# A two-layer backbone with 32 experts: layer 0's experts placed by rank, its router in batches

## The chip, the cores and the metric

The kernel runs on one core of a Trainium2 chip. The metric is the device time of one execution in microseconds (us); before the change its median is 3009.55 us over three runs (3004.5 to 3014.62).

## The reference

A stream of 512 latent tokens and 256 context tokens, 1024 wide, passes through two layers. Each layer has a modulated RMS norm, one input projection, three token mixers (a bidirectional recurrence, full attention, windowed attention), a gated sum, an output projection with a gated residual, and then the part that matters here:

```python
h2 = rms_norm(x, norm2_g) * (1 + scale) + shift        # modulation by c or c_ctx
group  = argmax(h2 @ w_group)                           # 1 of 4 groups
top2   = two largest of (h2 @ w_router) in that group   # 2 of 8 experts, softmax weights
y      = sum over the two: w * (silu(h2 @ gate_e) * (h2 @ up_e)) @ down_e
x      = x + gate * y
```

The group's softmax probability is a factor of the weights too. An expert has gate and up matrices of 1024 x 512 and a down matrix of 512 x 1024, all fp32. The output is the final norm of the 512 latent tokens. Layer 0 runs its experts for all 768 tokens, layer 1 for the 512 latent ones.

## The kernel before

**Router.** `out_proj` (lines 1075 to 1156) runs the output projection in two halves of 512 columns, over six token tiles in layer 0 and four in layer 1, three matmuls per k (tile `oo`). The second half's results are normalised in pairs of tiles; transposes (`xgt`) and logits (`lg`) are put off in a queue `steps`, of which `run(1)` takes one step per tile, and the rest of the router (`h2_out`, `route`, `route_pos`, `route_tab`) lies in a queue `later`, run after the last tile. For each token and choice the router works out the expert (`Er`), the token's position among that expert's tokens (`pos`, a matmul with a triangle of ones), and by a one-hot matrix `po` (L1317) a table `tab` (L1318) of 128 rows with the token number and the weight for each place. `ridx` (L1153) is that table as indices. The normalised rows go to DRAM (`h2D`): ScalarE scales, GpSimd adds the shift row (L1196), a DMA writes (L1198); the last tile's add is on VectorE (L1193), and its DMA on SyncE.

**Quads.** The experts run in eight quads. Quad q holds expert q of each of the four groups; each of these four has one of TensorE's four tiles of 32 columns. A plane gives each of the four 32 rows, so it is one gather of 128 rows of `h2D` (L1509, GpSimd), eight transposes, 64 gate matmuls, 64 up matmuls, a Silu (L1555) and a product, four transposes, 64 down matmuls (L1549), and a scatter that adds 128 rows to `xsD` in DRAM (L1514). `PLANES = (3, 2)` gives layer 0 three planes for every quad (96 places per expert) and layer 1 two (64). Tokens beyond that go through a loop at L1454 whose number of turns is read from `nx` into a register at L1453; it runs no turn here.

The order of work in a quad is: gate (both halves of the weights), down of the quad before, Silu, up, transposes of the next. Successive matmuls are written for the four column tiles in turn (`quad_mm`, `quad_down`); the order in which an engine gets its instructions is fixed when the kernel is built.

**Weights.** Each layer has 192 loads of 1 MiB, in the order of use, all on SyncE's queue (`ring_load`, L989). They fill slots in turn: 15 in layer 0, 16 in layer 1 (`wraw`, `pf`, `wspr`, `ring`). A load waits until TensorE has read what the slot held. The first 15 or 16 are issued during the projection and the router.

## Time and profile before

| | before |
|---|---|
| median of three runs | 3009.55 us |
| profiled execution | 3010.81 us, its span 3009.0 us |
| mean granted clock of TensorE | 0.972 |
| TensorE busy | 2822.9 us (94%) |
| VectorE, ScalarE, GpSimd busy | 1270.4, 835.1, 370.3 us |
| layer 0: last projection matmul, indices, quads left | 1024.9, 1070.3, 1699.1 us |
| layer 1: the same | 2446.4, 2475.6, 2976.9 us |

The busy time of an engine is the sum of its instructions, overlaps counted once. Matmuls are pipelined, so TensorE that is busy all the time need not run at its peak: the number of matmuls in a stretch tells more. "PEclk" is the granted clock, 1.00 is 2.4 GHz. "DMA share" is the mean busy share of the core's 16 DMA engines. In a timeline a row can gather several instructions of one kind (x8); the brackets behind it give the engine's idle time and what ended it. Names ending in q, as SPq, are an engine's instruction queue.

### The profile page before, as it was taken

How to read it: one execution, taken by the hardware profiler on the slowest of the kernel's cores; microseconds unless marked ns; L12 is line 12 of the kernel's file. 1: busy time of each engine (PE TensorE's matmuls, PEld its weight loads, DVE VectorE, ACT ScalarE, POOL GpSimd, SP SyncE). 2: the span in 40 equal slices, each digit the busy share in tenths (PEclk: the TensorE clock that was granted, in tenths of full speed). 3: DMA queues.
4: the chain of work that ended last, by engine and by line, in shares of the span. 5: the costliest groups of instructions: out<-in, count | busy, mean ns of one | idle time of the engine just before them, and what ended most of it. 6: DMA issues, size and time to landing. Idle time of an engine off the chain costs nothing. (4 is left out here: it accounts for less than half of the span.)

```text
span 3009.0 us, 49938 instructions
## 1 busy us (share of the span) xinstructions
PE 2822.9 (94%) x20898; PEld 1924.1 (64%) x20898; DVE 1270.4 (42%) x2693; ACT 835.1 (28%) x1706; POOL 370.3 (12%) x463
## 2 busy tenths in 40 slices
PE   6999999999999879999999799999999969999995
PEld 5999998888999733343333388888887853333321
DVE  5667555464446622221111356666566651110001
ACT  5322345555422200000000243335666221000000
POOL 1000221012212201111100100011001220100000
PEclk9999999999999889999999899999999979999998
DMA  6232334034555568998787612222112768999995
GB/s 237 70 112 96 119 105 138 25 104 169 189 206 191 199 255 342 385 377 353 290 326 293 227 50 74 91 95 75 48 40 82 272 248 358 409 416 414 416 414 198
DMA packets 198654, 640.07 MB, mean 213 GB/s; under 512 B 21585, under 2 KB 87377, under 8 KB 149273
## 3 DMA queue, kind: packets, MB, share of 16 engines
q1 hardware_dynamic: 165960, 552.59, 47.3%
q0 software_dynamic: 31744, 81.58, 8.7%
q8 instruction: 166, 2.72, 0.4%
q10 hardware_dynamic: 720, 2.66, 0.2%
q14 instruction: 64, 0.52, 0.0%
HBM read 600.44 MB, written 57.26 MB: 219 GB/s over the span
## 5 line engine op out<-in xcount | busy, mean ns | idle before, releaser
L503 PE MATMUL ga<-hhi,wsp 128*128 128x384 f32 (+1 forms) x1152 | 355.2, 372 | 4.4 <-ACT gt L950 2.8
L1537 PE MATMUL gu<-ring,xT 128*32 128x512 f32 x1824 | 331.1, 599 | 8.8 <-DMA ring<-in_w_exp_up 6.9
L1537 PE MATMUL gu<-wspr,xT 128*32 128x512 f32 x1328 | 290.2, 600 | 5.1 <-DMA wspr<-in_w_exp_up 3.9
L1537 PE MATMUL gu<-wraw,xT 128*32 128x512 f32 x1488 | 264.2, 604 | 1.6 <-DMA wraw<-in_w_exp_up 1.5
L1549 PE MATMUL dn<-ring,hT 128*32 128x512 f32 x1128 | 232.6, 595 | 0.0
L239 DVE TENSOR_TENSOR wsp<-wraw,wsp 128x1024 fp32r<-128x1024 f32 x148 | 183.3, 1241 | 115.4 <-ACT wsp L238 107.5
L503 PEld LDWEIGHTS ga<-hhi,wsp 128*128 128x128 f32 x1152 | 210.0, 189 | 23.5 <-ACT gt L950 4.4
L238 ACT ACTIVATE wsp<-wraw 128x1024 fp32r<-128x1024 f32 x148 | 155.9, 1058 | 176.6 <-PE bp L1026 89.9
L1537 PEld LDWEIGHTS gu<-ring,xT 128*32 128x32 f32 x1824 | 89.6, 110 | 177.7 <-issue 151.7
L503 PE MATMUL ga<-hlo,wsp 128*128 128x384 f32 (+1 forms) x576 | 191.3, 359 | 0.0
L1549 PE MATMUL dn<-wspr,hT 128*32 128x512 f32 x688 | 173.8, 596 | 0.0
L1026 PE MATMUL bp<-bhl,wsp 128*128 128x384 f32 (+1 forms) x864 | 167.7, 355 | 1.0 <-ACT bhl L1007 1.0
L1026 PEld LDWEIGHTS bp<-bhl,wsp 128*128 128x128 f32 x864 | 153.8, 188 | 14.5 <-issue 1.2
L1514 POOL DMA_INDIRECT xsD<-yr,ridx x40 | 63.5, 1588 | 761.8 <-DVE yr L1578 526.1
L1537 PE MATMUL gu<-pf,xT 128*32 128x512 f32 x480 | 155.0, 599 | 1.2 <-DMA pf<-in_w_exp_up 1.2
L245 PE MATMUL aacc<-wsp,hhi 128*128 128x256 f32 x512 | 149.9, 293 | 2.1 <-ACT gt L950 1.1
L1537 PEld LDWEIGHTS gu<-wraw,xT 128*32 128x32 f32 x1488 | 68.6, 111 | 123.5 <-issue 113.6
L1578 DVE SCALAR_TENSOR_TENSOR yr<-dn,wts,G 128x512 f32<-128x512 f32 x48 | 35.6, 749 | 260.4 <-PE dn L1549 231.8
L246 PE MATMUL aacc<-wsp,hhi 128*128 128x256 f32 x512 | 144.2, 282 | 0.7 <-DVE wsp L239 0.7
L1559 DVE TENSOR_TENSOR hs<-hs,gu 128x512 f32<-128x512 f32 x40 | 27.5, 687 | 277.8 <-PE gu L1537 270.9
L247 PE MATMUL aacc<-wsp,hlo 128*128 128x256 f32 x512 | 143.9, 282 | 0.0
L888 ACT ACTIVATE P<-S,nm 128x768 f32<-128x768 f32 (+3 forms) x160 | 120.4, 752 | 78.4 <-DVE nm L886 36.6
(352 smaller groups left out, 5536.9 us busy)
## 6 DMA issues: line engine op xcount, KB each, us to landing
ring<-in_w_exp_down SPq DMA_DIRECT2D x57, 1024.0 KB, 20.6
ring<-in_w_exp_up SPq DMA_DIRECT2D x51, 1024.0 KB, 15.0
wraw<-in_w_mod SPq DMA_DIRECT2D x46, 1024.0 KB, 7.7
wraw<-in_w_in SPq DMA_DIRECT2D x42, 1024.0 KB, 4.8
wraw<-in_w_exp_gate SPq DMA_DIRECT2D x40, 1024.0 KB, 13.7
ring<-in_w_exp_gate SPq DMA_DIRECT2D x39, 1024.0 KB, 22.9
wspr<-in_w_exp_gate SPq DMA_DIRECT2D x34, 1024.0 KB, 19.1
wraw<-in_w_exp_up SPq DMA_DIRECT2D x34, 1024.0 KB, 15.4
```

Source lines behind the costliest of these rows:

```text
L238: self.nc.scalar.activation(hv, src, AF.Copy)
L239: (self.nc.gpsimd if len(parts) in slow else self.nc.vector).tensor_tensor(lv, src, hv.bitcast(F32), op=OP.subtract)
L245: mm(out, l[0], r[0], start=start, stop=False)
L246: mm(out, l[0], r[1], start=False, stop=False)
L247: mm(out, l[1], r[0], start=False, stop=stop)
L503: mm(o, w(k)[wi][:, fs], self.h[hi_][:, k, a:a + s], start=k == 0 and wi == 0 and hi_ == 0, stop=k == 7 and wi == 1)
L888: nc.scalar.activation(P[:, :nk], S[:, :nk], AF.Exp, bias=nm[:, 0:1], accum_out=nm[:, 2:3])
L1026: nc.tensor.matmul(o[:, c, :step], w(k)[wi][:, fs], b[:, 4 * hi + k, c * step:(c + 1) * step], start=k == 0 and wi == 0 and hi == 0, stop= ...
L1514: self.nc.gpsimd.indirect_dma_start(out=self.xsD[L][:, :], out_offset=bass.IndirectOffsetOnAxis(ap=idx, axis=0), in_=y[:, :], in_offset=No ...
L1537: self.nc.tensor.matmul(o[c], xT[n][:, 4 * h + k, c], w(g, k), start=h + k == 0, stop=h * k == 3)
L1549: self.nc.tensor.matmul(b[c], h[:, k, c], w[k // 2](g, k % 2)[:, js], start=k == 0, stop=k == 3)
L1578: V.scalar_tensor_tensor(y[:, js], b, wt, G, op0=OP.mult, op1=OP.mult)
```

## The change

- **Ranks.** In layer 0 the experts of a group are placed in quads by rank: expert 0 stays in quad 0, and the others follow by falling number of tokens. The counts come from a matmul (`route_count`), the ranks from comparisons (`route_rank`). The table of the rank's owner, `ids`, is made by three operations on one partition and a cast.
- **Planes.** Layer 0 gets three planes in quads 0 to 2 and two in the rest, 19 instead of 24. Layer 1 keeps two. Tokens over 96 or 64 go to the overflow loop, now in blocks of 128.
- **Weights.** Layer 0's loads of quads 1 to 7 take the expert's number from a register of SyncE, one per place, 28 in all, read from `ids`. Quad 0's loads stay fixed.
- **Router.** It works on three tiles (two in layer 1) at a time. Logits of all tiles but the last are taken inside the projection's loop, and the first half's position matmuls too. The table matmuls come at the end: twelve in layer 0.
- **Rows of `h2D`.** The shift rows are written to DRAM beforehand; ScalarE scales in place, and a DMA that accumulates adds the rows. GpSimd's and VectorE's additions go.

```diff
-PLANES = (3, 2)
+PLANES = ((3, 3, 3, 2, 2, 2, 2, 2), (2,) * QUADS)
+CAP = 2 * UNIT
...
+        if i == 7:
+            ctx = CTX if L < DEPTH - 1 else 0
+            for a, r0, r1 in ((1, 0, ctx), (0, ctx, ctx + SEQ)):
+                if r1 > r0:
+                    row = self.modrow(L, a, 3)
+                    src = bass.AP(tensor=row.tensor, offset=row.offset, ap=[[0, r1 - r0], [1, D]])
+                    nc.gpsimd.dma_start(self.h2D[L][1 + r0:1 + r1, :], src)
...
+            def src(g):
+                if L or q == 0:
+                    e = w[8 * g + q]
+                else:
+                    if (q, g) not in self.ev:
+                        r = 4 * q + g
+                        self.ev[q, g] = self.nc.sync.value_load(self.ids[:1, r:r + 1], min_val=0, max_val=N_EXP - 1)
+                    e = w[bass.ds(self.ev[q, g], 1)].rearrange("a d f -> (a d) f")
...
                     for k in range(8):
                         self.mm3(b[:, :512], tuple(x[:, k, i * 128:(i + 1) * 128] for x in self.m), w(k), k == 0, k == 7)
+                        if k == 4:
+                            if half == 1 and i == nt - 1:
+                                self.route_pos(0, cut, R)
+                            run(2 if half == 1 and i == 1 else 1 if half or i > 1 else 0)
                     run(1)
...
+            self.h2_out(L, nt - 1, nt, R)
+            self.route(L, cut, nt, R)
+            self.route_pos(cut, nt, R)
+            if L == 0:
+                self.route_rank(p)
+            self.route_tab(L, cut if L else 0, nt, R)
...
+    def h2_out(self, L, i0, i1, R):
+        nc = self.nc
+        for i in range(i0, i1):
+            x = R["x"][self.ot[i]]
+            nc.scalar.activation(x, x, AF.Copy, scale=R["r"][:, i:i + 1])
+            nc.gpsimd.dma_start(self.h2D[L][i * 128 + 1:i * 128 + 129, :], x, accum_op=OP.add)
...
+        V.tensor_tensor(key, self.cnt, c[:, C_KM:C_KM + 32], op=OP.mult)
+        V.tensor_tensor(key, key, c[:, C_KC:C_KC + 32], op=OP.add)
+        g = p.tile([128, 32, 8], F32, name="kgt", tag="g2")
+        kg = key.rearrange("p (g j) -> p g j", j=8)
+        for i in range(4):
+            V.tensor_tensor(g[:, 8 * i:8 * i + 8], kg[:, i:i + 1].to_broadcast([128, 8, 8]), kg[:, i, :, None].to_broadcast([128, 8, 8]), op=OP.is_gt)
+        V.tensor_reduce(self.rk, g, axis=AX.X, op=OP.add)
...
-            order = [(q, n) for q in range(QUADS) for n in range(P)]
+            order = [(q, n) for q in range(QUADS) for n in range(P[q])]
...
-                S = [self.ps.tile([128, 512], F32, name="gu", tag="gu", bufs=6) for _ in range(P)]
+                S = [self.ps.tile([128, 512], F32, name="gu", tag="gu", bufs=6) for _ in range(P[q])]
```

Three places show how instructions move. On TensorE after layer 0's last out-projection matmul (`oo`), before, from the end of the logits (`lg`) to the first transpose of a gathered tile (`xtp`):

```order
L1206 MATMUL xgt<-cst,xo_9795 128x128 x4
L1214 MATMUL lg<-wr,xgT 128x36 x4
L1206 MATMUL xgt<-cst,xo_9797 128x128 x4
L1214 MATMUL lg<-wr,xgT 128x36 x8
L1277 MATMUL pos<-Ep,cst 128x64
L1279 MATMUL pos<-Es,cst 128x64
L1318 MATMUL tab<-rh,po 128x48 x4
L1277 MATMUL pos<-Ep,cst 128x64
L1279 MATMUL pos<-Es,cst 128x64
L1318 MATMUL tab<-rh,po 128x48 x4
```

and of the change, from inside the last tile's projection on:

```order
L1340 MATMUL pos<-Ep,cst 128x96
L1342 MATMUL pos<-Es,cst 128x96
L1262 MATMUL xgt<-cst,xo_9804 128x128 x4
L254 MATMUL oo<-wsp,mhi 128x512
L255 MATMUL oo<-wsp,mhi 128x512
L256 MATMUL oo<-wsp,mlo 128x512
```

```order
L1270 MATMUL lg<-wr,xgT 128x36 x4
L1262 MATMUL xgt<-cst,xo_9806 128x128 x4
L1270 MATMUL lg<-wr,xgT 128x36 x4
L1340 MATMUL pos<-Ep,cst 128x96
L1342 MATMUL pos<-Es,cst 128x96
L1358 MATMUL cnt<-Ep,cst 128x32
L1411 MATMUL tab<-rh,po 128x48 x12
L1626 MATMUL xtp<-cst,xo_9244 128x128 x8
```

Three rounds of positions and four table matmuls have become one round inside the projection, one after it, and twelve table matmuls at the end. On VectorE of the change, from the ranks (`rk`) to the one-hot matrices (`po`):

```order
L1374 SCALAR_TENSOR_TENSOR rk<-rk,cst 128x32
L1391 TENSOR_TENSOR Xr<-Er,rk 128x384
L1216 TENSOR_TENSOR idq<-rk,cst 1x1024
L1392 TENSOR_REDUCE rt<-Xr 128x12
L1217 TENSOR_TENSOR idq<-idq,cst 1x1024
L1394 TENSOR_TENSOR gq<-rt,cst 128x108
L1218 TENSOR_REDUCE idf<-idq 1x32
L1396 TENSOR_TENSOR Eq<-gq 128x96
```

The three operations of 1024 elements for `ids` stand among those that make the table. On SyncE, before, behind the last tile's rows:

```order
L1198 DMA h2D_95<-xo_9795 128x1024
L989 DMA ring<-in_w_exp_up 128x2048 x3
L989 DMA wraw<-in_w_exp_up 128x2048
L989 DMA wraw<-in_w_exp_gate 128x2048 x3
L989 DMA pf_9778<-in_w_exp_gate 128x2048
```

and of the change:

```order
L988 ISA x2
L1554 TENSOR_LOAD nx
L1554 ISA x2
L1019 DMA wraw<-in_w_exp_up 128x2048
L1019 ISA
L1019 DMA wraw<-in_w_exp_gate 128x2048
L1019 ISA
L1019 DMA wraw<-in_w_exp_gate 128x2048
```

The 28 reads of `ids` and the read of `nx` stand ahead of the first load that needs a freed slot, and each load by register has an instruction of its own beside it.

## Rows read from the trace of the kernel before

**Rows 1.** Stretches, experts: span, busy by engine (count), PEclk, DMA share, GB/s.

```profile
1081.00:1710.00 629.00, 612.80 (x4910) 216.15 (x4908) 116.35 (x207) 46.89 (x76) 59.28 (x47) 0.99 0.84 323
2488.00:2977.00 489.00, 467.70 (x3251) 153.70 (x3252) 51.22 (x102) 27.84 (x47) 34.44 (x26) 0.99 0.96 393
```

**Rows 2.** The same columns for windows of 100 us within these stretches.

```profile
1200.00:1300.00 100.00, 99.76 (x872) 35.68 (x876) 22.04 (x59) 9.45 (x16) 11.32 (x10) 1.00 0.98 394
1500.00:1600.00 100.00, 95.97 (x727) 32.69 (x722) 14.46 (x22) 5.92 (x10) 4.92 (x4) 0.98 0.78 301
2800.00:2900.00 100.00, 95.39 (x630) 30.02 (x630) 10.15 (x14) 4.56 (x8) 6.27 (x4) 1.00 1.01 411
```

**Rows 3.** Timeline of ScalarE, first Silu of a quad: start, us, instruction.

```profile
1098.66 0.60 ACT L1555 ACTIVATE hs<-gu 128x512 f32<-128x512 f32 x1 [12.76 <-PE gu L1537]
1147.82 0.60 ACT L1555 ACTIVATE hs<-gu 128x512 f32<-128x512 f32 x1 [2.99 <-PE gu L1537]
1217.79 0.60 ACT L1555 ACTIVATE hs<-gu 128x512 f32<-128x512 f32 x1 [2.93 <-PE gu L1537]
1288.99 0.60 ACT L1555 ACTIVATE hs<-gu 128x512 f32<-128x512 f32 x1 [2.93 <-PE gu L1537]
1443.62 0.60 ACT L1555 ACTIVATE hs<-gu 128x512 f32<-128x512 f32 x1 [3.29 <-PE gu L1537]
1616.82 0.60 ACT L1555 ACTIVATE hs<-gu 128x512 f32<-128x512 f32 x1 [13.27 <-PE gu L1537]
2849.83 0.60 ACT L1555 ACTIVATE hs<-gu 128x512 f32<-128x512 f32 x1 [10.83 <-PE gu L1537]
2912.78 0.60 ACT L1555 ACTIVATE hs<-gu 128x512 f32<-128x512 f32 x1 [14.65 <-PE gu L1537]
```

**Rows 4.** Line 1453, TensorE weight queue: ns min/median/max, first to last start.

```profile
L1453 PEldq EVENT_SEMAPHORE  x12: 51/51/51, 1699.1 to 2976.9; - x12
```

**Rows 5.** Columns as in rows 1: two down products of layer 0.

```profile
1230.00:1250.00 20.00, 20.00 (x192) 6.93 (x188) 8.86 (x12) 0.00 (x0) 3.64 (x2) 1.00 0.84 298
1460.00:1480.00 20.00, 20.00 (x129) 5.95 (x125) 6.43 (x9) 0.00 (x0) 2.59 (x2) 1.00 0.62 231
```

**Rows 6.** Line 1453 and timeline, SyncE: register read, first later loads.

```profile
L1453 SPq TENSOR_LOAD <-nx x2: 306/389/472, 1672.5 to 2952.1; - x2
...
1094.38 0.33 SPq L989 DMA_DIRECT2D wraw<-in_w_exp_up  x1
1095.18 1.60 SPq L989 DMA_DIRECT2D wraw<-in_w_exp_gate  x3
```

**Rows 7.** Timeline after layer 0's last out-projection matmul, TensorE, VectorE, GpSimd.

```profile
1024.46 0.40 PE L247 MATMUL oo<-wsp,mlo 128*128 128x512 f32 x1
1024.69 0.98 PE L1214 MATMUL lg<-wr,xgT 128*128 128x36 f32 x8
1025.50 1.07 PE L1206 MATMUL xgt<-cst,xo 128*128 128x128 f32 x8
1068.07 1.94 PE L1318 MATMUL tab<-rh,po 128*128 128x48 f32 x8 [2.85 <-DVE po L1317]
...
1032.97 2.80 DVE L1236 SCALAR_TENSOR_TENSOR t<-l,gm,cst 128x4 f32<-128x4 f32 x1
1053.28 1.28 DVE L1193 SCALAR_TENSOR_TENSOR xo<-xo,n2y,S 128x1024 f32<-128x1024 f32 x1
1070.27 0.18 DVE L1153 TENSOR_TENSOR ridx<-tab,z 128x24 int32<-128x24 f32 x1
...
1033.39 2.35 POOL L1196 TENSOR_TENSOR xo<-xo,S 128x1024 f32<-128x1024 f32 x1
```

**Rows 8.** Timeline, layer 1: last out-projection matmul, indices.

```profile
2445.96 0.40 PE L247 MATMUL oo<-wsp,mlo 128*128 128x512 f32 x1
...
2475.57 0.17 DVE L1153 TENSOR_TENSOR ridx<-tab,z 128x16 int32<-128x16 f32 x1
```

**Rows 9.** DMA issues of layer 0's experts: name, queue, count, median us to landing.

```profile
xsD<-yr,ridx POOLq DMA_INDIRECT x24, 8.3
```

More of the change, by code (lines that the diff above doesn't have):

```diff
@@ L36 @@
 UNIT = 32
[L37 removed]
 QUADS = 8
[L39 to L40 removed]
+PLANES = ((3, 3, 3, 2, 2, 2, 2, 2), (2,) * QUADS)
+CAP = 2 * UNIT
+BLOCK = 128
+MAX_EXTRA = 2 * T // (CAP + 1)
 FAR = float(1 << 20)
@@ L50 @@
 C_GO = C_R32 + 32
-C_W = C_GO + 32
+C_RK = C_GO
+C_KM = C_RK + 32
+C_KC = C_KM + 32
+C_GR = C_KC + 32
+C_W = C_GR + 32
 def host_consts():
@@ L1096, in out_proj @@
             R["ss"] = p.tile([128, NT, 2], F32, name="ssx")
+            R["r"] = p.tile([128, NT], F32, name="rn")
+            R["SW"] = p.tile([128, NT, 36], F32, name="SWt")
+            R["pl"] = p.tile([128, 2 * NT, 3], F32, name="plt")
+            R["pp"] = p.tile([128, 2 * NT], F32, name="ppt")
             R["tb"] = self.ps.tile([128, 512], F32, name="tab", tag="bg", bufs=1)
             wo = self.I["w_out"][L]
-            steps, later = deque(), deque()
+            steps = deque()
+            cut = nt // 2
+            sw = p.tile([2, 36], F32, name="sw")
             def run(k):
                 for _ in range(k):
-                    q = steps or later
-                    if q:
-                        q.popleft()()
+                    if steps:
+                        steps.popleft()()
             def logit_bias():
@@ new lines, in route @@
+        E = self.Er[:, i0:i1]
+        src = sel
+        v = []
+        for k in range(2):
+            v.append(tl([1], f"v{k}"))
+            V.reduce_max(v[k][:, :, 0], src, axis=AX.X)
+            q, m = tl([32], f"k{k}"), tl([1], f"m{k}")
+            V.tensor_tensor(q, src, bc(v[k], [32]), op=OP.is_equal)
+            V.tensor_tensor(q, q, bc(c[:, None, C_R32:C_R32 + 32], [32]), op=OP.mult)
+            V.reduce_max(m[:, :, 0], q, axis=AX.X)
+            V.tensor_tensor(E[:, :, k], q, bc(m, [32]), op=OP.is_equal)
+            if k == 0:
+                src = tl([32], "sel2")
@@ L1293, in route_pos @@
[L1293 to L1299 removed]
+        nc.tensor.matmul(b[:, :32 * n], c[:, C_TRI:C_TRI + 128], R["Es", i0].rearrange("p a e -> p (a e)"), start=False, stop=True)
@@ new lines, in route_pos, with route_count @@
+        V.tensor_tensor(R["pl"][:, 2 * i0:2 * i1], ge[:, :, 0:3], ge[:, :, 1:4], op=OP.subtract)
+        V.tensor_reduce(pn[:, :, 0], ge[:, :, 1:4], axis=AX.X, op=OP.add)
+        V.scalar_tensor_tensor(R["pp"][:, 2 * i0:2 * i1], pn[:, :, 0], -float(UNIT), pos, op0=OP.mult, op1=OP.add)
+    def route_count(self):
+        b = self.ps.tile([128, 512], F32, name="cnt", tag="tp")
+        self.nc.tensor.matmul(b[:, :32], self.c[:, C_ONE:C_ONE + 128], self.Ep[:, len(self.ot)], start=True, stop=True)
+        self.nc.vector.tensor_copy(self.cnt, b[:, :32])
@@ new lines, in route_rank @@
+    def route_rank(self, p):
+        V = self.nc.vector
+        c = self.c
+        self.route_count()
+        key = p.tile([128, 32], F32, name="key")
+        V.tensor_tensor(key, self.cnt, c[:, C_KM:C_KM + 32], op=OP.mult)
[5 more added lines that the diff above has]
+        V.tensor_reduce(self.rk, g, axis=AX.X, op=OP.add)
+        V.scalar_tensor_tensor(self.rk, self.rk, 4.0, c[:, C_GR:C_GR + 32], op0=OP.mult, op1=OP.add)
@@ L1314, in route_tab @@
-        for a in range(2):
-            for ch in range(2):
-                po = p.tile([128, 128], F32, name="po", tag="po", bufs=4)
-                V.tensor_scalar(po, c[:, C_IO:C_IO + 128], self.tgt[:, i + a, ch:ch + 1], None, op0=OP.is_equal)
-                nc.tensor.matmul(R["tb"][:, :48], po, rh[:, a, ch].rearrange("p a b n -> p (a b n)"),
-                                 start=i + a + ch == 0, stop=last and a + ch == 2)
+        n = i1 - i0
+        m = 2 * n
+        last = i1 == len(self.ot)
@@ new lines, in route_tab, with tl @@
+        bufs = 1 if L == 0 else 2
+        w = 2 * NT if L == 0 else 4
+        def tl(shape, name):
+            return p.tile([128, w] + shape, F32, name=name, tag=name, bufs=bufs)[:, :m]
+        rt = self.rt[:, 2 * i0:2 * i1]
+        rk = c[:, C_RK:C_RK + 32] if L else self.rk
+        X = tl([32], "Xr")
+        V.tensor_tensor(X, self.Er[:, i0:i1].rearrange("p a c e -> p (a c) e"), rk[:, None, :].to_broadcast([128, m, 32]), op=OP.mult)
+        V.tensor_reduce(rt, X, axis=AX.X, op=OP.add)
@@ new lines, in route_tab @@
+        V.tensor_tensor(rh[:, :, 1], Df, self.wt2[:, i0:i1].rearrange("p a c -> p (a c)")[:, :, None].to_broadcast([128, m, QUADS * 3]),
+                        op=OP.mult)
+        for a in range(m):
+            po = p.tile([128, 128], F32, name="po", tag="po", bufs=4)
+            V.tensor_scalar(po, c[:, C_IO:C_IO + 128], tgt[:, a:a + 1], None, op0=OP.is_equal)
+            nc.tensor.matmul(R["tb"][:, :48], po, rh[:, a].rearrange("p b n -> p (b n)"),
+                             start=i0 + a == 0, stop=last and a == m - 1)
@@ L1431, in moe @@
                     self.quad_down(L, p, hT, q - 1, need)
-                hs_ = [self.exp_s(S[n], 128) for n in range(P)]
-                U = [self.ps.tile([128, 512], F32, name="gu", tag="gu", bufs=6) for _ in range(P)]
+                hs_ = [self.exp_s(S[n], 128) for n in range(P[q])]
+                U = [self.ps.tile([128, 512], F32, name="gu", tag="gu", bufs=6) for _ in range(P[q])]
                 self.quad_mm(U, xT, need((1, q, 0)), 0)
@@ L1436, in moe @@
                 if q + 1 < QUADS:
-                    xT = [next_x() for _ in range(P)]
+                    xT = [next_x() for _ in range(P[q + 1])]
                 prev = [self.exp_m(h, u, 128) for h, u in zip(hs_, U)]
```

267 lines of the change are left out of this document (133 added, 134 removed).

## The prediction

> **What bounds the kernel now.** I read the table of stretches first. The experts of layer 0 (1081 to 1710 us) are the longest stretch that the change touches: TensorE is busy 612.8 of 629 us and the DMA engines are busy 0.84 of the time [rows 1]. The same eight quads in layer 1, with two planes instead of three, take 489 us at a DMA share of 0.96. The 100 us windows say it more sharply [rows 2]: in 2800:2900 the DMA share is 1.01 at 411 GB/s with TensorE idle for 4.6 us, in 1200:1300 both are nearly full, in 1500:1600 TensorE has no time left and the DMA is at 0.78. So layer 1 waits for weights, and layer 0 starts with both close to their limits and ends with TensorE alone as the bound.
>
> The timeline of the Silu, one per plane as soon as a quad's gate matmuls are done, gives the pace [rows 3]. Layer 0's first Silus of quads 0, 1, 2, 3, 5 and 7 stand at 1098.66, 1147.82, 1217.79, 1288.99, 1443.62 and 1616.82: steps of 49.2, 70.0 and 71.2, then 154.6 and 173.2 for two quads each, 77 and 87 for one. TensorE leaves the quads at 1699.1 [rows 4], 82.3 after the last of them: 600.4 in all. Layer 1 goes at 62.9 (2849.83 to 2912.78) and leaves 64.2 after its last Silu, at 2976.9.
>
> Why do layer 0's late quads take 77 to 87 and not 71? In 1230:1250 TensorE does 192 matmuls in 20 us, in 1460:1480 only 129, both at full clock [rows 5]. The first are the down products of an early quad, written so that successive matmuls go to the four column tiles in turn; in the late ones the built order puts several for one tile behind each other (two or three with the same weight slot). The late order costs 192 x (20/129 - 20/192) = 9.8 us for a three-plane down product. That accounts for most of the 6 to 16.
>
> **The planes.** The change takes 5 of 24 planes from layer 0, all in quads 3 to 7. A step from Silu q to Silu q+1 holds down(q-1), up(q) and gate(q+1), so I go step by step.
> - 0 to 1 and 1 to 2 keep three planes everywhere and the built order of before: 49.2 and 70.0.
> - 2 to 3 loses one plane of gate(3), 64 matmuls at 9.6 per us, 6.7, and eight transposes, some 1.6: 71.2 - 8.3 = 62.9.
> - 3 to 4 has two planes of up and gate but down(2) of three, now in the slow order: 192/6.45 = 29.8; 256 matmuls at 8 per us (my estimate between the two rates of [rows 5]) 32.0; transposes about 5. That is 66.8.
> - 4 to 5, 5 to 6, 6 to 7 and what follows have the work of layer 1, whose built order of column tiles they also have. There the step is 62.9 and the tail 64.2. Layer 0 has 15 weight slots and layer 1 has 16, so that a load can be issued a little later; I take 64.5 and 65.
>
> The sum is 49.2 + 70.0 + 62.9 + 66.8 + 3 x 64.5 + 65 = 507.4, against 600.4: 93 us less. From the low side, if weights never were late, a two-plane step would be the 62.9 of layer 1 less the 21.3 us that its TensorE is idle in 489, spread on eight quads: 60.2, and 15 us more gain. From the high side, if two-plane quads in layer 0 took the 70.0 of its own three-plane step, the sum would be 49.2 + 70.0 + 70 + 72 + 3 x 70 + 70 = 541: a gain of 59.
>
> A rule speaks against 62.9. The windows of layer 1 move 411 GB/s [rows 2], and 24 loads of 1 MiB at that rate are 61.2 us, close to the step. The Trainium skill's page "DMA: Bandwidth & Descriptors" (Specifications) gives about 358 GB/s as the limit of HBM for one core; by it 24 loads would take an estimated 70.3 us and the gain would be the 59 of the high side. The trace does not agree with it, in any window of layer 1, so I leave that case a chance and do not take it.
>
> **Weights by register.** From quad 1 on, layer 0's loads take their expert from one of 28 registers, filled from the table of ids by SyncE. Before has a read of this kind: 306 to 472 ns at L1453 [rows 6], with two short instructions behind it; with these I count 0.65 us, so 28 are 18 us. They stand behind the ids, some 8 us before the indices of the gathers, and behind them stands only the load for the first slot to come free. Before issues that load 24.1 us after the indices are ready (1094.38 against 1070.27). From ids to that load there are then 32 us for 18 us of reads: they cost nothing. Were that cover gone, each us late would idle the DMA queue by a us, at most 18. The read of the overflow count moves ahead of these loads too; its value is ready soon after the indices. Each load gets one more register instruction. Three loads without it take 1.60 us to issue (0.53 each); with a whole register read on each of them, the nearest row, it would be 1.2 us, or 28 us for 24 loads, still under the 63 us of a quad. From below it costs nothing. I take nothing.
>
> **The router in layer 0.** The last out-projection matmul ends at 1024.86, the indices come at 1070.27 [rows 7]: 45.4 us. Eight sets of logits stand behind that matmul in before; in after only one does. The other seven run inside the projection, where TensorE is saturated, so they push its end out by 7 x (0.81 + 0.53) = 9.4 us (a logit set from 1024.69 to 1025.50; four transposes at half of 1.07 for eight). Behind it I count from the built order: three vector operations of 0.69 and then transposes, copy and logits, 5.4; some 26 dependent small vector operations at about 0.2, 5.2; positions 1.1; the rank (13 operations) 3.4; from there to the first one-hot matrix 6.9, of which three operations of 1024 elements on one partition are 3.8 by the nearest row, the 1.28 at 1053.28; twelve table matmuls at 1.94/4 each, 5.8; the last two operations and their wait 1.9. Sum 29.7. What goes are the additions on GpSimd, 2.35 each [rows 7], beside which VectorE's 128x4 operations take 2.80 instead of 0.2. The gain is 45.4 - 9.4 - 29.7 = 6.3. From the low side, if each small operation cost 0.4, it is -2; from the high side, with 0.15, about 9. One wait is new: the position matmuls of tiles 0 to 2 stand inside the last projection tile, and its remaining matmuls queue behind them. After the routing of these tiles is issued TensorE has 36 matmuls of 0.23 [rows 7] and three logit sets before them, 12 us; VectorE has about 32 small operations and two output tiles, 10 to 11. I take no stall, and up to 5 us as the end.
>
> **The router in layer 1.** From 2446.36 to 2475.57 are 29.2 us [rows 8]. Five sets move into the projection, 6.7; behind it the same chain without the rank and with four table matmuls is about 18. Gain 4.5, with -3 and 7 as ends. The rows of the last tile are now added to DRAM by an accumulating transfer: the nearest row is the accumulating scatter, 8.3 us to landing [rows 9]. Norm, scale and issue, 6.5 by the same count of operations, and 8.3 make 14.8, under the 18 of the indices, behind which the gathers wait on GpSimd. In layer 0 there are 15 us of margin. The shift rows prefilled into DRAM are issued long before on GpSimd; what waits behind them there is nothing on the path.
>
> **The sum.** 3010.81 (the profiled execution, 1.3 above the median of 3009.55) - 93 - 6.3 - 4.5 = 2907.0, or 2906 by the median. I put 2907.
>
> **Rivals.**
> - *TensorE stays the bound with no wait for weights.* Layer 0 pays 600.4/24 = 25.0 us for a plane, so five planes would be 125 less: 3010.8 - 125 - 10.8 = 2875. For it: layer 0's late windows with DMA share 0.78 and all of TensorE. Against: 50 us for a quad needs 503 GB/s, and no window shows over 411. It can hold only while the slots' lead lasts, so 2875 is an end, not a centre. Chance 0.12.
> - *The transfer takes over early.* Layer 0's two-plane quads stand at 70 each, by the rate of the worst loads or the fewer slots: 3010.8 - 59 - 10.8 = 2941. For it: windows of layer 0 in which the DMA stands at 1200:1300's 0.98 and 394 GB/s. Against: layer 1 does this work in 62.9. Chance 0.15.
> - *The router gives nothing.* Logits within the projection, a long chain by rank and the one-partition operations eat the 10.8: 2918. For it: all those operations are in one chain behind the last tile. Against: the stalls of 2.3 to 2.8 us have no cause left. Chance 0.13.
> - *Slower: register-fetched loads become the bound.* On SyncE's queue each of the 168 loads would need a time t, and a quad 24t. From t = 63/24 = 2.6 us on this sets the pace; the gain of 104 is gone at 24t = 63 + 104/7 = 78, t = 3.2 us. At 4 us a quad is 96, and the kernel takes 2907 + 7 x 33 = 3138. Against it stand 0.53 for a load and 0.65 for a register read; for it only that no row shows a load whose address comes from a register. Chance 0.05.
> - *The change doesn't do what it says.* An expert of quads 3 to 7 in layer 0 with over 64 tokens would go through the overflow loop, six serial loads per turn. The reference's inputs give at most 59 there (and 82 in the three-plane quads), so no turn runs. Chance 0.01, put with the slower side.
>
> **Numbers.** The forecast, with its own range 2892 to 2925, has 0.54; it and the router's rival lie at 2890 to 2930. The range that holds 8 in 10 goes from 2875 (all of TensorE's pace) to 2943 (the transfer's). No change within 0.3%, 9 us, about what a measurement of this kernel can tell, would need a t near 3.2: 0.01. Faster 0.94, slower 0.05.
>
> **What will show it.** Silus of layer 0 with steps near 49, 70, 63, 67 and 64 to 65, with DMA share of 0.95 or more in the last three quads and waits for weights there. 192 matmuls in 20 us in the early down products and about 129 in the late. Twenty-eight register reads on SyncE that end before the first load is due; loads by register issued within 1 us. Indices 30 us after the last projection matmul in layer 0, 18 in layer 1, the projection longer by 9 and 7, and no vector operation of 128x4 above 0.5 us. If the two-plane steps are under 58, or the first load comes later than 25 us behind the indices, or the layer 1 quads change at all, the reasoning is wrong there.

## The result, and the profile after

The change takes 2937.45 us (median of four runs, 2932.54 to 2944.39), the kernel before 3010.24 in the runs beside it: a ratio of 0.9766, 95% interval 0.9749 to 0.9783. The forecast was 2907; its range, 2875 to 2943, holds the time near its upper end, the narrower one of 2892 to 2925 does not. About 73 us were gained of the 104 forecast. The profiled execution took 2932.54 with a span of 2930.8, the fastest of its four.

Where the time went, from the two profiled executions (us, minus is gained):

| stretch | before | after | forecast | measured |
|---|---|---|---|---|
| start to layer 0's first out-projection matmul | 950.0 | 959.7 | 0 | +9.7 |
| layer 0's out projection | 74.9 | 85.2 | +9.4 | +10.3 |
| last matmul of it to the indices | 45.4 | 27.3 | -15.7 | -18.1 |
| indices to first Silu | 28.4 | 28.6 | 0 | +0.2 |
| first Silu to the end of the quads | 600.4 | 511.9 | -93 | -88.5 |
| to layer 1's first out-projection matmul | 693.4 | 695.5 | 0 | +2.1 |
| layer 1's out projection | 53.9 | 59.1 | +6.7 | +5.2 |
| last matmul of it to the indices | 29.2 | 17.6 | -11.2 | -11.6 |
| indices to first Silu | 23.7 | 32.3 | 0 | +8.6 |
| layer 1's quads | 477.7 | 482.3 | 0 | +4.6 |
| the end | 32.1 | 31.3 | 0 | -0.8 |

The profiled execution lies 25.5 us above the forecast. Four rows make it up: the start (9.7), layer 1 from the indices to the first Silu (8.6), layer 1's quads (4.6) and layer 0's (4.5); the others together are 1.9 better than forecast.

The rows of after, as in the groups of before. ScalarE's timeline, first Silu of quads 0 and 2 to 7 of layer 0 (start, us, instruction):

```profile
1100.78 0.60 ACT L1656 ACTIVATE hs<-gu 128x512 f32<-128x512 f32 x1 [12.77 <-PE gu L1638]
1219.79 0.60 ACT L1656 ACTIVATE hs<-gu 128x512 f32<-128x512 f32 x1 [2.93 <-PE gu L1638]
1287.38 0.60 ACT L1656 ACTIVATE hs<-gu 128x512 f32<-128x512 f32 x1 [2.93 <-PE gu L1638]
1369.99 0.60 ACT L1656 ACTIVATE hs<-gu 128x512 f32<-128x512 f32 x1 [14.72 <-PE gu L1638]
1421.82 0.60 ACT L1656 ACTIVATE hs<-gu 128x512 f32<-128x512 f32 x1 [10.21 <-PE gu L1638]
1483.06 0.60 ACT L1656 ACTIVATE hs<-gu 128x512 f32<-128x512 f32 x1 [10.88 <-PE gu L1638]
1548.91 0.60 ACT L1656 ACTIVATE hs<-gu 128x512 f32<-128x512 f32 x1 [15.08 <-PE gu L1638]
```

With quad 1's at 1149.95 the steps are 49.2, 69.8, 67.6, 82.6, 51.8, 61.2 and 65.8, where 49.2, 70.0, 62.9, 66.8 and three of 64.5 were forecast [rows 3]; the tail is 63.8, 65 forecast. The table of stretches for quad 3's step and the three behind it (columns as in rows 1):

```profile
1287.00:1370.00 83.00, 74.60 (x526) 27.23 (x522) 17.81 (x43) 4.71 (x9) 8.87 (x7) 0.96 0.96 379
1370.00:1422.00 52.00, 51.74 (x409) 19.54 (x404) 8.41 (x12) 3.70 (x7) 4.22 (x3) 1.00 1.02 405
1422.00:1483.00 61.00, 57.88 (x412) 18.68 (x408) 8.41 (x12) 3.29 (x6) 3.15 (x2) 1.00 1.02 408
1483.00:1549.00 66.00, 61.10 (x400) 18.15 (x395) 7.03 (x10) 2.37 (x5) 3.11 (x2) 1.00 1.02 410
```

In the last three the DMA share is 1.02 at 405 to 410 GB/s, as full as layer 1 had it [rows 2]. In the last two of them TensorE is idle for 3 and 5 us, mostly until a weight load has landed: the weights set the pace there. In 1370 to 1422 it is idle for 0.3 of 52 us, so that this short step is TensorE's own pace for two planes; the run with late tables, below, shows that it goes with the long step before it. In 1287 to 1370 TensorE lost over 8 us and its mean clock was 0.96. Quad 2's step, which came out 4.7 longer than forecast, of the change and before:

```profile
1219.80:1287.40 67.60, 67.36 (x584) 23.89 (x580) 15.30 (x31) 4.78 (x9) 7.22 (x5) 1.00 0.98 384
1217.80:1289.00 71.20, 70.96 (x624) 25.73 (x620) 16.02 (x32) 5.32 (x10) 8.31 (x6) 1.00 0.96 383
```

It has 40 matmuls fewer, not the 72 of the forecast.

The quads end here (TensorE's weight queue, as in rows 4):

```profile
L1554 PEldq EVENT_SEMAPHORE  x12: 51/51/51, 1612.7 to 2899.5; - x12
```

SyncE's reads of the registers, and its first loads behind them [rows 6]:

```profile
L988 SPq TENSOR_LOAD <-ids x28: 262/263/471, 1065.7 to 1081.2; - x28
```

```profile
1096.49 0.34 SPq L1019 DMA_DIRECT2D wraw<-in_w_exp_up  x1
1097.30 1.63 SPq L1019 DMA_DIRECT2D wraw<-in_w_exp_gate  x3
```

Twenty-eight reads take 16 us, 18 were forecast; they end at 1081.7, and the first load goes at 1096.49, 24.3 us after the indices (24.1 before). Three loads by register are issued in 1.63 us, 1.60 before. Behind layer 0's last projection matmul [rows 7]:

```profile
1044.55 0.39 PE L256 MATMUL oo<-wsp,mlo 128*128 128x512 f32 x1
1066.62 5.35 PE L1411 MATMUL tab<-rh,po 128*128 128x48 f32 x24 [8.93 <-DVE po L1410]
...
1060.50 1.21 DVE L1216 TENSOR_TENSOR idq<-rk,cst 1x1024 f32<-1x1024 f32 x1
1072.22 0.18 DVE L1208 TENSOR_TENSOR ridx<-tab,z 128x24 int32<-128x24 f32 x1
```

The indices come 27.3 us later, 29.7 were forecast, with the one-partition operations at 1.21 each and the twelve table matmuls in 5.35. No operation of this chain waits for GpSimd any more.

**The trunk.** The first surprise lies at 295 us, where the forecast had not looked. Timelines of GpSimd, VectorE and ScalarE in the change, and two of its DMA issues between 290 and 330 us (name, KB, median us to landing):

```profile
292.64 1.23 POOL L309 DMA_DIRECT2D h2D<-modD  x2 [3.69 <-DMA modD<-mmr]
293.86 1.15 POOL L284 DMA_DIRECT2D mbr<-in_b_mod  x2
...
311.14 0.29 DVE L300 SCALAR_TENSOR_TENSOR mmr<-macc,mbr 128x128 f32<-128x128 f32 x1 [8.97 <-DMA mbr<-in_b_mod]
...
314.58 2.00 ACT L247 ACTIVATE wsp<-wraw 128x1024 fp32r<-128x1024 f32 x2 [14.07 <-DMA wraw<-in_w_in]
...
h2D<-modD POOLq DMA_DIRECT2D x1, 1024.0 KB, 17.4
mbr<-in_b_mod POOLq DMA_DIRECT2D x2, 4.0 KB, 16.8
```

The shift rows, 2 MB and 1 MB from DRAM to DRAM, are issued in the middle of the trunk. A 4 KB load behind them lands after 16.8 us (4.9 before in the same stretch), VectorE waits 9.0 us for it, and ScalarE 14.1 for a weight load. From TensorE's first `kv` matmul behind 250 us to the last before 330 us it takes 71.7 us, 62.8 before: 8.9 us lost.

**Quad 3.** VectorE and TensorE:

```profile
1326.64 1.41 DVE L1679 SCALAR_TENSOR_TENSOR yr<-dn,wts,G 128x512 f32<-128x512 f32 x2 [6.15 <-DMA xsD<-yr,ridx]
...
1329.97 0.66 PE L1474 MATMUL ovt<-rho,poo 128*128 128x46 f32 x2 [4.27 <-DVE rho L1473]
1331.62 0.63 PE L1474 MATMUL ovt<-rho,poo 128*128 128x46 f32 x2 [0.99 <-DVE rho L1473]
1333.04 0.66 PE L1474 MATMUL ovt<-rho,poo 128*128 128x46 f32 x2 [0.79 <-DVE rho L1473]
```

VectorE wants to write the third plane's output tile and has to wait for the scatter of the first, since there are two buffers. Behind it stand the overflow tables; TensorE's table matmuls wait for them, and quad 3's up matmuls queue behind. In the whole step TensorE waits 8.1 us at tables. That order of instructions put a stall of VectorE, harmless by itself, on TensorE's path.

**Layer 1's gathers.** TensorE, GpSimd and VectorE from the last projection matmul on [rows 8]:

```profile
2366.94 0.40 PE L256 MATMUL oo<-wsp,mlo 128*128 128x512 f32 x1
2398.66 1.94 PE L1626 MATMUL xtp<-cst,xo 128*128 128x128 f32 x8 [14.00 <-DMA xo<-h2D,ridx]
2402.79 1.94 PE L1626 MATMUL xtp<-cst,xo 128*128 128x128 f32 x8 [2.19 <-DMA xo<-h2D,ridx]
2404.66 8.99 PE L1638 MATMUL gu<-wraw,xT 128*32 128x512 f32 x64
...
2375.57 0.85 POOL L1254 DMA_DIRECT2D h2D<-xo  x1 [4.93 <-ACT ge L1321]
...
2384.91 0.17 DVE L1208 TENSOR_TENSOR ridx<-tab,z 128x16 int32<-128x16 f32 x1
2387.69 0.17 DVE L1440 COPY ovy<-pos 128x8 f32<-128x8 f32 x1 [2.53 <-DMA h2D<-xo]
```

The accumulating write of the last tile is issued at 2375.57 and has landed by 2387.69; GpSimd starts the gathers at 2388.42, 3.5 us behind the indices, and they take 10 us to land. First gate matmul 19.8 us behind the indices, 12.4 before.

### The profile page after: what moved, and what is told of

The parts are those of the page before. It is cut to its first block, busy times and chain, and to the rows that moved or that the text cites. A ratio compares the mean times of both kernels' runs of the same rounds, so it can differ in the third digit from the quotient of the medians.

```text
span 2930.8 us, 48158 instructions
## 1 busy us (share of the span) xinstructions
PE 2720.3 (93%) x19874; PEld 1876.1 (64%) x19874; DVE 1237.7 (42%) x2633; ACT 827.9 (28%) x1691; POOL 342.4 (12%) x447
## 3 DMA queue, kind: packets, MB, share of 16 engines
q0 software_dynamic: 31488, 86.29, 10.3%
## 5 line engine op out<-in xcount | busy, mean ns | idle before, releaser
L1638 PE MATMUL gu<-ring,xT 128*32 128x512 f32 x1568 | 283.9, 594 | 13.5 <-DMA ring<-in_w_exp_up 11.5
L1638 PE MATMUL gu<-wspr,xT 128*32 128x512 f32 x1152 | 253.9, 600 | 8.2 <-DMA wspr<-in_w_exp_up 6.3
L1638 PE MATMUL gu<-wraw,xT 128*32 128x512 f32 x1320 | 237.8, 601 | 6.1 <-DMA wraw<-in_w_exp_up 4.5
L1650 PE MATMUL dn<-ring,hT 128*32 128x512 f32 x1000 | 204.8, 595 | 0.0
L1638 PEld LDWEIGHTS gu<-ring,xT 128*32 128x32 f32 x1568 | 74.5, 109 | 165.4 <-issue 127.9
L1669 ACT ACTIVATE hT<-htp 128x512 f32<-128x512 f32 x35 | 19.9, 596 | 513.8 <-PE htp L1668 513.7
L1660 DVE TENSOR_TENSOR hs<-hs,gu 128x512 f32<-128x512 f32 x35 | 24.1, 688 | 319.6 <-PE gu L1638 313.0
L1650 PE MATMUL dn<-wspr,hT 128*32 128x512 f32 x576 | 145.9, 596 | 0.0
L1638 PEld LDWEIGHTS gu<-wraw,xT 128*32 128x32 f32 x1320 | 59.9, 110 | 124.4 <-issue 103.4
L1615 POOL DMA_INDIRECT xsD<-yr,ridx x35 | 55.5, 1587 | 705.4 <-DVE yr L1679 504.2
L1638 PE MATMUL gu<-pf,xT 128*32 128x512 f32 x440 | 135.6, 595 | 0.9 <-DMA pf<-in_w_exp_up 0.9
```

The lines of the kernel that those rows point to most:

```text
L1615: self.nc.gpsimd.indirect_dma_start(out=self.xsD[L][:, :], out_offset=bass.IndirectOffsetOnAxis(ap=idx, axis=0), in_=y[:, :], in_offset=No ...
L1638: self.nc.tensor.matmul(o[c], xT[n][:, 4 * h + k, c], w(g, k), start=h + k == 0, stop=h * k == 3)
L1650: self.nc.tensor.matmul(b[c], h[:, k, c], w[k // 2](g, k % 2)[:, js], start=k == 0, stop=k == 3)
L1660: self.nc.vector.tensor_tensor(hs[:C], hs[:C], U[:C], op=OP.mult)
```

## The experiments

Each is the change with one edit, unless said otherwise, timed beside the kernel before; the ratio to compare with is 0.9766 (0.9749 to 0.9783). Layer 0's quads are counted here from the first Silu to the register read behind them, 0.7 us past the mark of the table: 512.6 us in the change, 601.1 before. Five versions that leave these quads as they are, the change among them, lie at 512.6 to 513.6: that is the scatter of this number.

**Shift rows issued from the merge's code.**

```diff
-        if i == 7:
...
-                    nc.gpsimd.dma_start(self.h2D[L][1 + r0:1 + r1, :], src)
...
+                nc.gpsimd.dma_start(self.h2D[L][1 + r0:1 + r1, :], src)
```

> The two DMAs that write the shift rows to DRAM (2 MB and 1 MB for layer 0) are issued at the start of the merge instead of in the middle of the trunk. Theory A: these writes sit on GpSimd's queue ahead of a 4 KB load of the modulation's bias, which VectorE waits for (9.0 us in the trace of the change) and TensorE behind it; with the writes gone from there the out projection of layer 0 starts near 950 instead of 959.7, and the kernel takes about 2928 (8 to 10 us less than the change's 2937). Rival B: the 9.7 us come from the transfer of 3 MB itself, wherever it stands; then the out projection moves by less than 3 us, or the merge gets longer by as much, and the time stays within 3 us of 2937.

Measured 2940.46, ratio 0.9763 (0.9745 to 0.9781): no change. The edit did not do what was meant: the scheduler left the two DMAs in the trunk, at 294.76 (292.64 in the change), but now behind the loads of the bias. That tells the parts apart. GpSimd and ScalarE:

```profile
289.47 2.20 POOL L284 DMA_DIRECT2D mbr<-in_b_mod  x4
294.76 1.24 POOL L1024 DMA_DIRECT2D h2D<-modD  x2 [3.09 <-DMA modD<-mmr]
...
315.88 2.00 ACT L247 ACTIVATE wsp<-wraw 128x1024 fp32r<-128x1024 f32 x2 [13.70 <-DMA wraw<-in_w_in]
```

The bias is there in time, and TensorE still loses 10 us, by a weight load 13.7 us late. So it is not the place in GpSimd's queue; it is the traffic of 3 MB while the trunk's weights come just in time. Theory A's mechanism fell; rival B's "wherever it stands" is not tested, since the DMAs did not move to the merge.

**Shift rows spread over the merge**, six DMAs of 128 rows, each tied behind one of the merge's loads.

```diff
-        if i == 7:
...
+                        ins = nc.gpsimd.dma_start(g[:, :n], self.gtD[L][br * 8 + dt, :, :n])
+                        i = (br * 8 + dt) // 4
+                        if dt &3 == 2 and i < len(self.ot):
...
+                            with tc.issue_after(ins.ins):
+                                nc.gpsimd.dma_start(self.h2D[L][1 + i * 128:129 + i * 128, :], src)
```

> Six (layer 1: four) DMAs of 128 shift rows each instead of two of 256 and 512 rows, each issued on GpSimd behind one of the merge's loads, so that none runs in the trunk. In the run before, the two DMAs stayed at 295 us, now behind the bias loads, and TensorE still lost 10 us there, this time for a weight load (13.7 us). Theory A: what costs the 10 us is the traffic of these writes at a place where the trunk's weights are just in time; spread over the merge they are hidden, the out projection of layer 0 starts at 950 to 954, and the kernel takes 2925 to 2930. Rival B: the merge and the out projection lose as much; the kernel stays within 3 us of 2937.

Measured 2928.75, ratio 0.9731 (0.9716 to 0.9746), 9 us less: theory A's range. Two stretches of the change, and the same two of this kernel (columns as in rows 1):

```profile
300.00:320.00 20.00, 12.42 (x99) 11.06 (x99) 8.77 (x16) 4.23 (x7) 2.30 (x4) 0.83 0.86 223
965.00:985.00 20.00, 17.91 (x95) 14.13 (x94) 10.21 (x13) 3.26 (x8) 12.06 (x17) 1.00 0.73 240
```

```profile
300.00:320.00 20.00, 19.80 (x230) 18.29 (x219) 12.61 (x25) 7.60 (x12) 3.78 (x7) 1.00 0.64 201
965.00:985.00 20.00, 16.89 (x81) 13.50 (x80) 5.61 (x9) 2.25 (x6) 6.48 (x6) 0.79 0.60 189
```

In 300:320 TensorE runs 230 matmuls instead of 99, and layer 0's out projection starts at 951.9 instead of 959.7. The projection itself takes 90.9 instead of 85.2 us: in 965:985 the granted clock is 0.79, half speed (1.2 GHz) for most of 976 to 987, behind 3.0 us in which TensorE was idle in 965:976. So 7.9 were won there and 5.7 lost; the indices come 2.2 earlier. The four versions with spread rows start the projection at 949.3 to 952.4, the eight with the rows in the trunk at 956.6 to 963.2, so the gain there is clear of scatter. The loss is not tied to the rows: three of the four take 90.2 to 90.9 us for the projection, the fourth (all four edits, below) 85.5. The rest of the 9 between the medians cannot be placed from one profile of each, since the change's profiled run was its fastest.

**Overflow tables in quads 5 to 7.**

```diff
-                if q:
+                if q == 1 or q > 4:
                     for _ in range(2):
                         next(ovf, None)
```

> The overflow tables of layer 0 are made in quads 5 to 7 (two planes) instead of quads 2 to 4. In the trace of the change quad 3's step is 82.6 us, with TensorE waiting 7.6 us at the table matmuls, behind VectorE, which waits 6.2 us for the scatter of an output tile. Theory A: the step falls to about 72, but the next one rises from 51.8 to about 60, since the weights then set the pace: the eight quads together gain 2 to 5 us, the kernel takes 2932 to 2936. Rival B: the stall is lost time; the quads gain 8 us or more and the kernel takes about 2928.

Measured 2934.47, ratio 0.9746 (0.9730 to 0.9763). First Silus of quads 3 to 5:

```profile
1282.24 0.60 ACT L1656 ACTIVATE hs<-gu 128x512 f32<-128x512 f32 x1 [2.93 <-PE gu L1638]
1349.85 0.60 ACT L1656 ACTIVATE hs<-gu 128x512 f32<-128x512 f32 x1 [10.27 <-PE gu L1638]
1416.53 0.60 ACT L1656 ACTIVATE hs<-gu 128x512 f32<-128x512 f32 x1 [14.72 <-PE gu L1638]
```

Quad 3's step is 67.6, the forecast's 66.8; the next is 66.7 instead of 51.8. The quads take 510.0 instead of 512.6. From quad 3's first Silu to the register read they take 325.8, 326.0 in the change: of the 15 us won in the step nothing is left, and 2.4 of the 2.6 in the sum lie in quad 2's step (65.1 instead of 67.6), which lost its tables too. Theory A held in the sum, with the give-back it forecast. The medians of the whole kernel, 3 us apart, are not told from scatter.

**A third buffer for the output tile**, in place of one of `hT`.

```diff
-            y = p.tile([128, D], F32, name="yr", tag="yr", bufs=2)
+            y = p.tile([128, D], F32, name="yr", tag="yr", bufs=3 - L)
...
-        hT = p.tile([128, 4, C], F32, name="hT", tag="hT", bufs=4)
+        hT = p.tile([128, 4, C], F32, name="hT", tag="hT", bufs=3)
```

> The change with three buffers instead of two for the output tile yr in layer 0 (paid for with one hT buffer less). Theory A: VectorE's wait for the scatter of a quad's first plane when it wants to write the third (6.2 us at 1326.6 in the change's trace) goes, and with it most of TensorE's wait at the overflow tables: quad 3's step falls from 82.6 to 70 to 74. The next steps give back all but 2 to 5 us, since the weights set the pace there: quads about 508 to 510 us, the kernel 2932 to 2936. Rival B: the step stays above 80, because the tables and the slow order of the down product set it and not the wait.

Measured 2927.59, ratio 0.9733 (0.9720 to 0.9747). In quad 3's step VectorE no longer waits for the scatter; the step is 77.9, between the theories, and the quads take 509.7. TensorE still waits 4.1 us at the tables, where it and VectorE wait for each other by turns. That does not explain the 10 us to the 67.6 of the late tables; the rest is work of TensorE (73.5 us busy in this step, 67.0 there). The sum agrees with the run before: some 3 us. The median is 10 under the change's, below theory A's range; the profiled executions differ by 3.3, and the rest is not placed.

**Fixed addresses.** All loads at expert q of each group, so the weights are not those of the experts chosen.

```diff
-                if L or q == 0:
+                if True:
```

> The change with all loads of layer 0 at fixed addresses: the 28 register reads and the register addresses go. The loads fetch expert q of each group for quad q, so the weights are not those of the experts that the tokens chose. Theory A: the reads are done before the first load is due (the trace of the change shows that load 24.3 us after the indices, as before), and a load by register costs no more than another: the time is within 4 us of 2937. Rival B: register addresses slow the loads (DMA share 1.02 at 405 to 410 GB/s in layer 0's last quads against 411 to 418 in layer 1 before); the kernel takes 2925 or less.

Measured 2932.42, ratio 0.9747 (0.9732 to 0.9763), which the change's interval overlaps; 5 us less, just outside theory A's 4, and far from rival B's 2925. The quads take 512.9 us, with the registers 512.6. Reads and register addresses cost nothing that shows in the quads; the 5 us between the medians lie elsewhere (the out projection starts 2.8 earlier) and are not told from scatter.

**Three planes in all eight quads.**

```diff
-PLANES = ((3, 3, 3, 2, 2, 2, 2, 2), (2,) * QUADS)
+PLANES = ((3,) * QUADS, (2,) * QUADS)
```

> The change with three planes in all eight quads of layer 0 (24 planes as before; experts still placed by rank, weights by register, router in batches). Theory A: the planes are worth nearly the whole gain; without them layer 0's quads take 595 to 605 us as before and the kernel takes 3010 to 3030, no faster than before, since the router's gain in layer 0 is paid back by the trunk's 9.7 us and the gathers of layer 1. Rival B: the router is worth the 11 us forecast and the planes the rest: about 3000.

Measured 3020.53, ratio 1.0032 (1.0021 to 1.0043): 10 us slower than before. Layer 0's quads take 603.1 us, 512.6 in the change. Theory A held: five planes are worth 83 us by the medians (90 in the quads), and all the rest of the change cost 10.

**The same with the shift rows spread over the merge.**

> Three planes in all quads of layer 0 and the shift rows spread over the merge: the batched router, ranks and register loads without the fewer planes and without the traffic in the trunk. With three planes and that traffic it was 3020.5, 1.0032 of the kernel before. Theory A: the traffic was 9 of those 11 us, and what is left of the router is within 3 us of nothing: 3008 to 3014, 0.999 to 1.001 of the kernel before. Rival B: the router's batches cost time themselves: 3016 or more.

Measured 3011.47, ratio 1.0006 (0.9995 to 1.0017). Theory A held: the traffic was 9 of the 10 us, and the rest of the change, the batched router above all, is worth nothing that can be measured, where 10.8 were forecast. The profile of this run against before says where it went. In layer 0 the indices come 18.1 us sooner behind a projection 15.6 longer, which holds the slow-clock stretch seen in the run with spread rows. In layer 1 they come 11.7 sooner behind a projection 5.8 longer, and the way from the indices to the first Silu is 6.2 longer; the quads add 4.1.

**The last tile's rows by VectorE and a plain DMA on SyncE**, as before the change.

```diff
...
+            if i == len(self.ot) - 1:
+                nc.vector.scalar_tensor_tensor(x, x, R["r"][:, i:i + 1], R["S2"], op0=OP.mult, op1=OP.add)
+                nc.sync.dma_start(self.h2D[L][i * 128 + 1:i * 128 + 129, :], x)
+                continue
...
```

The last tile's rows are left out of those written beforehand, and its shift row is loaded for VectorE.

> The last token tile's rows are made as in the kernel before: one addition on VectorE and a plain DMA on SyncE, in both layers; the first ring loads stand behind it on SyncE again. In the trace of the change, layer 1's gathers start 3.5 us behind the indices and land 10 us later, after 8.2 in the kernel before, and the first gate matmul comes 19.8 us behind the indices instead of 12.4. Theory A: the accumulating DMA of the last tile (issued 2375.6, landed 2387.7) and the six ring loads issued before it are the cause; here layer 1's first gate matmul comes 12 to 14 us behind the indices and layer 1 gains about 5 us net of 1.3 for the addition: 2932 to 2934. Rival B: the gathers are slow because of the weights' traffic alone; no gain, within 2 us of 2937.

Measured 2932.19, ratio 0.9740 (0.9727 to 0.9753), which the change's interval overlaps. Layer 1's first gate matmul comes 16.8 us behind the indices, not 12 to 14, and the indices 1.7 later: 36.0 us from the last projection matmul, 37.3 in the change. But the versions that leave this part of layer 1 alone scatter as much: their first gate matmul comes 17.3 to 20.0 us behind the indices, 34.9 to 37.6 behind the projection. So no gain is shown, and theory A's cause is not shown either. The gathers still land late (xtp 10.9 us behind the indices, 8.6 before), which may be the six ring loads, issued 10 us ahead of the indices and not 15 as before. That was not settled.

**Two planes in quad 0**, whose experts have 42 to 58 tokens.

```diff
-PLANES = ((3, 3, 3, 2, 2, 2, 2, 2), (2,) * QUADS)
+PLANES = ((2, 3, 3, 2, 2, 2, 2, 2), (2,) * QUADS)
...
```

The limits in the overflow count follow.

> Planes (2, 3, 3, 2, 2, 2, 2, 2) in layer 0: 18 instead of 19. Quad 0 holds expert 0 of each group, with 42 to 58 tokens, so two planes hold them. Theory A: the weights set the pace of the eight quads once they flow; with quad 0 short they start to flow earlier: the first step falls from 49 to 33, of which the three-plane quads give back a part; the quads take 490 to 500 us from the first Silu instead of 512.6, and the kernel about 2915 to 2925. Rival B: TensorE sets the pace in the first four quads; a plane is worth its 17 to 25 us: 2912 to 2920, with a first step of 33 and the others unchanged. Rival C: the weights set the pace everywhere and a plane in quad 0 is worth nothing: 2935 or more.

Measured 2934.39, ratio 0.9743 (0.9729 to 0.9756). The first step falls to 37.2, but the third rises from 67.6 to 92.1; the fourth falls from 82.6 to 67.4, and the quads take 517.5 instead of 512.6. The time is nearly rival C's (2935 or more), but not for its reason: the stall at the tables has moved from quad 3 to quad 2 (VectorE waits 6.3 us for the scatter, TensorE 3.8 for the first table), and what the plane gained is gone with it. In 1130:1200 and 1200:1270 of this kernel:

```profile
1130.00:1200.00 70.00, 69.24 (x583) 25.44 (x578) 9.78 (x14) 6.35 (x11) 6.27 (x5) 1.00 1.02 408
1200.00:1270.00 70.00, 64.11 (x442) 21.21 (x444) 12.80 (x29) 2.99 (x5) 6.79 (x5) 0.95 0.84 316
```

At first the DMA is full, then, in the stretch in which TensorE stands, at 0.84.

**All four edits at once**: the diffs of the spread rows, the plain last tile, the late tables and the two planes in quad 0.

> All four edits at once: shift rows spread over the merge, last tile's rows plain, overflow tables in quads 5 to 7, planes (2, 3, 3, 2, 2, 2, 2, 2). If they add up: 10 + 4 + 3 + 17 us less than the change, about 2903. If the quads are set by the weights, the tables' edit is worth nothing beside the plane's, and it is 2906 to 2912.

Measured 2921.88, ratio 0.9702 (0.9689 to 0.9716): the best version, 15.6 us under the change, but above both forecasts (2903, and 2906 to 2912). The profiles of the two say where the sum fell short. The spread rows brought their 10.1 us before the projection. In layer 0's quads the two edits together brought 16.5 of 20 (first Silu 5.0 earlier behind the indices, quads 501.1 instead of 512.6), where the plane alone had lost 1 (first Silu 3.6 earlier, quads 4.9 longer): with the tables late its stall is gone. The plain last tile brought nothing clear of scatter. And from layer 0's quads to layer 1's out projection this version takes 703.1 us, 695.5 in the change: 7.6 lost. Layer 1's spread rows lie in that stretch, but by themselves they go with 697.4 and 695.3; no run tells the cause.

**All four and the third buffer.**

> The four edits of the run with all of them (2921.9 us), and three buffers for the output tile. There the step behind the two-plane quad and the three-plane quads took 77.4 us, with a wait of 6.4 us for the scatter, and layer 0's quads 501.1 us. Theory A: the wait is what is left of TensorE's stalls in these quads; the step falls to about 70 and the quads to 495 to 498, since the weights are not yet the limit there (the DMA share in that stretch was under 0.95): 2915 to 2919. Rival B: the weights set the pace of the sum; no change, 2920 to 2924.

Measured 2924.36, ratio 0.9714 (0.9699 to 0.9729); quads 501.6, 501.1 without it. Rival B's number: the wait of 6.4 us is gone, the third step stays 77.4. The table of stretches shows why (third step without the third buffer, then with it, and a later stretch with it):

```profile
1195.00:1272.00 77.00, 76.10 (x575) 26.72 (x569) 12.51 (x18) 5.14 (x9) 7.90 (x6) 1.00 0.96 373
1195.00:1270.00 75.00, 74.21 (x562) 26.21 (x564) 11.83 (x17) 5.16 (x9) 6.81 (x5) 1.00 0.96 373
1340.00:1400.00 60.00, 56.57 (x420) 20.16 (x414) 11.39 (x26) 3.33 (x6) 4.23 (x3) 1.00 1.02 407
```

TensorE is busy all through the third step either way: with the tables late, VectorE's wait held up nothing on its path, so theory A's premise was wrong. Nor is it the weights alone that set this step, as rival B has it: TensorE does not stand in it and the DMA share is 0.96; only later does TensorE wait, at 1.02.

## Why the prediction was right, and where it was wrong

**The planes: right, and for the reason given.** 88.5 of 93 us. The late two-plane quads run with full DMA, the early quads are unchanged at 49.2 and 69.8. The three-plane run shows that the planes are the whole gain. The rival in which TensorE stays the bound is refuted by the DMA share of 1.02 with TensorE idle in the late quads, the one with 70 per quad by the steps. The Trainium skill's page "DMA: Bandwidth & Descriptors" (Specifications) gives about 358 GB/s as the limit for one core. The trace does not agree: these quads ran at 405 to 410. The forecast named a two-plane step under 58 as a sign that the reasoning is wrong. There is one, 51.8, but only behind the long step before it: with late tables it is 66.7.

**The step 2 to 3: miscounted.** The forecast took 64 gate matmuls and 8 transposes out of it and got 62.9; the trace lost 40 and took 67.6. The last 32 gate matmuls of each plane run one plane behind the other, so that quad 2's first Silu leaves two planes' pieces behind it and quad 3's only one: the step loses 32 gate matmuls, not 64. At the forecast's 9.6 per us the other 32 are 3.3 of the 4.7.

**The step 3 to 4: mis-sized.** The slow down product was right, if a little short: its 192 matmuls stand between 1289.7 and 1322.1, around eight transposes, 32.3 us for the 29.8 taken. What I missed was the chain scatter, VectorE, overflow tables, TensorE in the new order, which the sum had at nothing. The step came out 15.8 longer; without its tables it is 67.6. From this step to the end of the quads that cost nothing, as the late tables show: the loads ran on while TensorE stood, and the next step took 51.8.

**Registers: right.** 16 us of reads under cover, no cost that shows in the quads. The slower rival is out.

**The router: the count was right, the balance wrong.** Chains of 27.3 and 17.6 against 29.7 and 18, projections of +10.3 and +5.2 against +9.4 and +6.7. Up to the indices the router gained 7.8 in layer 0, 6.3 forecast, and 6.4 in layer 1, 4.5 forecast; what takes it back lies elsewhere.

**The step that failed** is the sentence that the shift rows are "issued long before on GpSimd; what waits behind them there is nothing on the path". They cost 9 to 10 us in the trunk. What waited behind them on GpSimd's queue was the bias, on the path by 9.0 us; and with the bias ahead of them their bytes alone cost as much. With the rows spread over the merge 8.7 of the 30 us between forecast and median come back, and in the three-plane pair 9 of 10.

**Layer 1's gathers: mis-sized.** The forecast had the last tile's rows in DRAM 14.8 us behind the projection, 6.5 to the issue and 8.3 for the transfer. They were issued after 8.2 and took 12.1 to land, among six weight loads that no longer stood behind a DMA on SyncE's queue: 20.4, behind the indices instead of ahead of them. That these loads are the cause is not shown. From the indices to the first Silu the versions of the change take 29.1 to 32.6 us, 23.7 before. Behind the last projection matmul the indices come 11.6 us earlier, the first gate matmul only 4.3, and the projection is 5.2 longer. So the number of the rival "the router gives nothing" is what the router came to, 1.0006 with the traffic out of the way, but not by its mechanism: logits and chains cost about what was forecast, and the gathers of layer 1 and a slow-clock stretch in layer 0's projection ate the gain.

**The range: in part luck.** Its upper end, 2943, stood for a transfer that holds the two-plane quads at 70 us each. The time came to 2937 for other reasons, the shift rows and layer 1, for which the sum had nothing.

**What stays open.** Layer 1's quads take 4.6 us more. Up to the register read they are 481.9 to 482.6 in every version of the change, 477.8 in the one profile of before. The forecast named any change there as a sign of being wrong; there is one. The DMA's rows over 300 us of them, of the change (2470 to 2770) and of before (2550 to 2850):

```profile
DMA packets 18925, 122.78 MB, mean 409 GB/s; under 512 B 3377, under 2 KB 3377, under 8 KB 4532
q1 hardware_dynamic: 16169, 117.75, 94.7%
```

```profile
DMA packets 19105, 124.09 MB, mean 414 GB/s; under 512 B 3397, under 2 KB 3397, under 8 KB 4552
q1 hardware_dynamic: 16352, 119.09, 94.7%
```

The same loads run 1.2% slower with a full DMA. No run tells why.

## What to carry to other kernels

Work moved "ahead, where it is free" has bytes: ask of each new transfer what else the DMA engines have to deliver in the microseconds after it, and tie it to a place, since the order in the code does not hold it. Where a ring of buffers feeds a transfer-bound loop, a stall or a gain of the engine can be given back in the next step or two, so judge a step by the sum of its neighbours. And a shorter chain gains only what the next wait in line leaves of it.
